# Weight rests of 100 tiles: a subtraction on GpSimd replaced by an adding transfer onto a negated copy

## The chip, the cores and the metric

The kernel runs on one core of one Trainium2 chip. The time of a kernel is the device time of one execution in microseconds; of several executions the median is given. A second number, the span, goes from the first to the last instruction that the profiler recorded. Positions "at 1490.60" are microseconds from the start of the span of the profiled execution.

The engines are TensorE (PE in the rows: matrix products; PEld: its loading of the stationary operand), VectorE (DVE), ScalarE (ACT), GpSimd (POOL) and SyncE (SP, which here issues loads). Transfers (DMAs) run on 16 DMA engines, whoever issues them.

## The reference

Two layers of a diffusion trunk work on 256 latent tokens and 256 context tokens of width 1024, all in float32. Each layer is

```python
x  = x  + 0.5 * gate * rms(swiglu(modulate(rms(x))))      # macaron half step
x  = x  + gate * rms(concat(attention, s5, conv) @ w_out) # token mixer
x  = x  + 0.5 * gate * rms(swiglu(modulate(rms(x))))      # macaron half step
```

with `swiglu(h) = (silu(h @ wg) * (h @ wu)) @ wd`, inner width 2816. Shift, scale and gate come from products of a conditioning vector with `w_ada`. The context tokens go through the same layers up to the mixer of the last one, and the latent tokens of the last layer are the output.

## The kernel before, in words

**Products in three passes.** The matmuls take float32r operands. Each float32 operand is split into a rounded part and a rest: `hi = round(w)`, `lo = w - hi`. A product of weights and activations is then three matmuls, hi x hi, hi x lo and lo x hi, summed in PSUM (`mm3`, line 148; all of its matmuls carry line 158). `mmr` does the same with the activations as the stationary operand (line 493).

**Splitting a weight tile** (`wsplit`, lines 129 to 137). A tile is 128 partitions by 1024 columns (896 or 640 for the down projection). SyncE loads it into a raw buffer `wr` (line 126). ScalarE writes the rounded part `wh` (line 133). Then the rest `wl` is subtracted on VectorE or, with `pool` set, on GpSimd (line 136). There are 4 raw buffers, 6 buffers of `wh` and 6 of `wl`; a buffer is free again when its last reader is done. So SyncE can load about four tiles ahead, and a rest can be made as soon as the matmuls of a tile six before it are over.

**Who subtracts what.** GpSimd subtracts the gate and up tiles of the first feed-forward group of a macaron step (`weights`, line 619, through `units` of the interleaved projection), the down tiles of its last group (`down`, line 667), the first eight tiles of the mixer's input projection (line 1275), all of the output projections (`weight`, line 1303, and `rows_out`, line 1338), and the gate and up tiles of the last feed-forward (`ffn_last`, from line 499). VectorE subtracts the others.

**Order of the work.** TensorE's order is written out by hand. The tokens are handled in two spans of 256 columns. A macaron step goes through four groups of inner blocks, 5, 5, 5 and 7; each makes its gated activations and then its share of the down projection. In the last group this is done span by span: when the first span is summed, its normalization begins (`boundary`, line 379, and `pre`, line 356) while TensorE goes on with the second span. In it VectorE multiplies, adds to the stream `x` (line 392, for d = 0 and 4 on GpSimd) and adds squares up (`square_acc`, line 354; ScalarE makes the squares, line 353). TensorE sums over partitions (`ss`, line 340), VectorE works out the reciprocal root on 128x1 and 128x2 columns (lines 296 to 324), TensorE spreads it (`rb`, line 333), and VectorE and ScalarE form the next sublayer's input `hh`, `hl` (lines 365 to 373). Below, the stretch from the last group of one sublayer to the dense part of the next is called a handover; there are four before the last feed-forward.

**Interleaved projection** (`skewed`). The first tiles of the next sublayer are taken in units of two. The first two units go through the eight input blocks together, block by block, so that they can start when the first block of the new input is there; the other units follow one by one. For the second span three units are still in their buffers; the first one is loaded and split again at the end.

The order of VectorE, ScalarE, GpSimd and SyncE is laid out at compile time by a list scheduler that reckons with its own durations; each engine then works in that order, and each instruction waits for the semaphores that it needs. Background streams (products with `w_ada`, the state space tables) are put between, and are paused in the handovers.

Of the kernel before, what the change touches and what calls it, by code (L numbers as in the profile page):

```python
# [8 lines left out]
F32 = mybir.dt.float32  # L9
# [3 lines left out]
AF = mybir.ActivationFunctionType  # L13
OP = mybir.AluOpType
# [17 lines left out]
RF = -27.0 / 1024  # L32
MAGIC_ROUND = 12582912.0
RAW = 4
WB = 6
FIRST = 3
SKEW_IN = 4
# [2 lines left out]
PO = (0, 1)  # L40
PI = (0, 1)
# [39 lines left out]
class Trunk:  # L81
    def __init__(self, ctx, tc, a, out):
# [7 lines left out]
        self.small = P("small", 2)  # L90
        self.wpool = P("w", WB)
        self.mm = P("mm", 6, space=PSUM)
# [31 lines left out]
    def wraw(self, src, cols=1024):  # L124
        w = self.wpool.tile([128, 1024], F32, name=self.nm("wr"), tag="wr", bufs=RAW)
        self.nc.sync.dma_start(w[:, :cols], src)
        return w

    def wsplit(self, src, cols=1024, pool=False):
        nc = self.nc  # L130
        w = self.wraw(src, cols)
        h = self.wpool.tile([128, 1024], F32R, name=self.nm("wh"), tag="wh")
        nc.scalar.activation(h[:, :cols], w[:, :cols], AF.Copy)  # L133
        lo = self.wpool.tile([128, 1024], F32R, name=self.nm("wl"), tag="wl")
        eng = nc.gpsimd if pool else nc.vector
        eng.tensor_tensor(lo[:, :cols], w[:, :cols], h.bitcast(F32)[:, :cols], op=OP.subtract)  # L136
        return h, lo

    def split(self, x, lo, hi, pool=False):
# [431 lines left out]
    def skewed(self, units, H, pend, done):  # L571
# [4 lines left out]
        for i, (span, q) in enumerate(pend):  # L576
            self.drain(q)
            lo, hi, s = span
            use = [n for n, u in enumerate(units) if s in u[1]]
            have = list(W)[-(WB // 2):] if i else []  # L580
            use = [n for n in have[::-1] if n in use] + [n for n in use if n not in have]
# [19 lines left out]
    def ffn(self, l, j, H, pend, nxt, order=None):  # L601
        nc, a = self.nc, self.a
# [3 lines left out]
        for gi, fs in enumerate(FGROUPS):  # L606
# [10 lines left out]
                nc.vector.tensor_tensor(gl[:, lo:hi], g, gh.bitcast(F32)[:, lo:hi], op=OP.subtract)  # L617

            def weights(f, pool=True):
                return [self.wsplit(a["wgu"][l, j, i, f], pool=pool and i in PI) for i in range(2)]  # L620

            def gate_up(f, ws, lo, hi, late=False):
                ps = [self.ps("pgu") for _ in range(2)]
# [5 lines left out]
            if gi == 0 and not isinstance(pend, list):  # L629
                rest = fs[FIRST:]  # L630
                new = lambda s: self.wpool.tile([128, 1024], F32R, name=self.nm(s), tag=s)
                ws = [((new("wh"), new("wl")), a["wgu"][l, j, i, f]) for f in fs[:FIRST] for i in range(2)]
                with self.in_order(*ORDERED):
                    for k, hook in enumerate(pend(H, ws)):
                        if k == 0:
                            held = [self.ps("pgu") for _ in ws]
                        for n, (p, w) in enumerate(zip(held, ws)):
                            self.mm3(p, w[0], [H[k]], 0, T, [k], k == 0, k == KD - 1)
                            hook(n)
                    self.setup2()  # L640
                for n, f in enumerate(fs[:FIRST]):
                    glu(f, held[2 * n], held[2 * n + 1], 0, T)
            elif gi == 0:
                rest = fs[SKEW_IN:]
                units = [(lambda f=f: weights(f), (0, 1)) for f in fs[:SKEW_IN]]
                self.skewed(units, H, pend, lambda n, p, span: glu(fs[n], p[:, :256], p[:, 256:], *span[:2]))
            if gi == 0:
                self.pause = False
            for f in rest:
                ws = weights(f, gi == 0 and f != fs[FIRST] * FD)  # L650
                gate_up(f, ws, *((order or spans)[0][:2] if f == NF - 1 else (0, T)))
# [4 lines left out]
            lastg = gi == len(FGROUPS) - 1  # L656
# [9 lines left out]

            def down(d):
                return self.wsplit(a["wd"][2 * l + j, d, :, fs[0] * 128:(fs[-1] + 1) * 128], n * 128,
                                   pool=lastg and d % 2 in PO)

            def downs(ds, lo, hi):

                for ks in (range(n - 1), range(n - 1, n)):
                    for d in ds:
                        if not ks.start:
                            if d not in wd:
                                wd[d] = down(d)
                            pd[d] = self.ps("pd")
                        self.mm3(pd[d], wd[d], acts[ks.start:ks.stop], lo, hi, ks, ks.start == 0, ks.stop == n)
# [13 lines left out]
            for span in order or spans:  # L693
                lo, hi, _ = span
                ds = range(KD)
                if out:
                    gate_up(fs[-1], ws, lo, hi, True)
                    ds = ds[::-1]
                    for d in ds[WB - 2:]:
                        del wd[d]  # L700
# [40 lines left out]
    def ssm_params(self):  # L741
# [25 lines left out]

        pw = self.wpool.tile([128, 1024], F32, name=self.nm("pw"), tag="wr", bufs=RAW)[:, :2 * 9 * w]
        pw = pw.rearrange("p (i k w) -> p i k w", i=2, k=9)
# [223 lines left out]
    def ssm_chunks1(self, u):  # L993
# [3 lines left out]
        for half in range(2):  # L997
            t = self.wpool.tile([128, 1024], F32, name=self.nm("ut"), tag="wr", bufs=RAW)
            for jh in range(2):
# [77 lines left out]
    def ssm_out(self, l, gh, U, S, lo):  # L1077
# [6 lines left out]
        vt = [self.wraw(self.V[l, gh, ri]) for ri in range(2)]  # L1084
        yt = self.wpool.tile([128, 1024], F32, name=self.nm("yt"), tag="wr", bufs=RAW)
        ng, r = 128 // n, 8 * n // 128
# [139 lines left out]
    def mixer(self, l, H, pend, newH):  # L1226
        nc, a = self.nc, self.a
        last = l == NL - 1
        both = self.spans
        lo = CTX if last else 0  # L1230
# [30 lines left out]
        def conv(h):  # L1261
# [5 lines left out]
            for slo, shi, _ in (both[1:] if last else both):  # L1267
# [4 lines left out]
            nc.gpsimd.tensor_tensor(o[:, lo:], o[:, lo:], ev[8 + h][:, lo:], op=OP.mult)  # L1272
            cat[4 + h] = self.split(o, lo, T)

        units = [(lambda t=t: [self.wsplit(a["w_in"][l, t + i], pool=i in PI) for i in range(2)],
                  (1,) if last and t >= 4 else (0, 1)) for t in range(0, 8, 2)]

        def done(n, p, span):
# [22 lines left out]
        wo, po, ny, H2, out = {}, {}, ([], []), [], []  # L1301

        def weight(d):
            wo[d] = self.wsplit(a["w_out"][l, d], pool=True)

        def part(d, k, s):

# [28 lines left out]
        wr, yr, us, q = {}, {}, [], []  # L1336

        def rows_out(t, h, k):

            i = [k in z for z in KPAIRS].index(True)  # L1340
            if (h, i) not in wr:
                wr[h, i] = self.wsplit(a["w_outr"][h, i], pool=True)
            p, done = yr.setdefault((t, h), ([], []))
            if not p:
                p.append(self.ps("yr"))
            self.mmr(p[0], cat[k], wr[h, i], t, KPAIRS[i].index(k) * 512, not done, len(done) == KD - 1)
            done.append(k)
# [12 lines left out]
        units = [(i, qt) for i in range(4) for qt in ((0, 1) if last else (0, 1, None))]  # L1360
# [8 lines left out]
        def early_out(n):  # L1369
            if last:  # L1370
                rows_out(n // 100, n // 10 % 10, n % 10)
            else:
                part(n // 100, n // 10 % 10, n % 10)
# [5 lines left out]
            t=tile_in, u=lambda n: ut.extend(self.ssm_chunks1(u)), U=lambda n: U.extend(self.ssm_chunks2(ut)),  # L1379
            v=lambda n: vtok(), k=lambda n: ksplit(), q=qsplit,  # L1380
            s=lambda n: S.append(self.ssm_states(l, n, U)), o=lambda n: yt.append(self.ssm_out(l, n, U, S[n], lo)),
            b=lambda n: G.append(self.ssm_back(yt[n], lo)), w=weight, r=lambda n: next(rows, None),
            g=lambda n: self.ssm_glu(l, G, cat, lo), e=early_out, x=tail if last else bound, S=attn_s,
            y=lambda n: oevac(n // 10, n % 10), z=lambda n: self.advance(out[0][1]), W=weight,
            T=lambda n: PT.update({n: self.attn_t(P.pop(n), units[n][1])}),
            V=lambda n: self.attn_pv(PT.pop(n), vt, cat, *units[n]))
# [243 lines left out]
```

## Time and profile before

| | us |
|---|---|
| median of 3 executions | 1874.86 |
| lowest, highest | 1871.24, 1876.22 |
| profiled execution, its own time | 1868.04 |
| its span | 1866.3 |

The mean granted clock of TensorE over the span is 0.963 of 2.4 GHz. The row of a group of instructions gives the line, the engine, the operation, its output and inputs by the program's names, their shapes, the number of instructions, the busy time and the mean duration of one. A row of a timeline gives start and duration and, in brackets, the idle time of the engine before it and what ended that. A row of the chain of waits gives start, duration and what the end of the program depended on in that time. The table by stretches gives, for each engine, busy microseconds in a window with the number of instructions, then TensorE's granted clock, the mean busy share of the DMA engines and what they moved.

### The profile page before, as it was taken

What the parts mean: (1) busy time and instruction counts of PE and PEld (TensorE: products, weight loads), DVE (VectorE), ACT (ScalarE), POOL (GpSimd) and SP (SyncE); (2) the same over time, 40 slices, a digit from 0 to 9 for tenths busy, and PEclk for the clock granted to TensorE, in tenths of its full rate; (3) what the DMA queues carried; (4) which work ended last, traced back from release to release, by engine and by line L of the source; (5) the groups of instructions that cost most, each with busy time, mean ns of one, the idle gap of its engine ahead of it and who ended that gap; (6) DMA issues with size and microseconds to landing.
All of it is one profiled execution on the core that took longest, in us unless ns stands there. A gap on an engine that the chain in (4) does not pass through costs nothing.

```text
span 1866.3 us, 28704 instructions
## 1 busy us (share of the span) xinstructions
PE 1728.9 (93%) x11040; PEld 1490.1 (80%) x11040; DVE 1244.4 (67%) x2204; ACT 667.2 (36%) x1181; POOL 730.6 (39%) x647
## 2 busy tenths in 40 slices
PE   7999989977997989999999979999999879889998
PEld 5887768867976889777888979888888878679997
DVE  5787877578669676767874386765456696964334
ACT  4432222224334553322222243322222334455443
POOL 4100978745354143443438353000001553436552
PEclk9999989988998989999999989999999999899999
DMA  7665556553143121655664332656466423455662
GB/s 277 223 197 170 181 154 208 192 175 102 45 154 131 34 79 47 189 182 170 199 194 156 108 102 63 209 162 199 125 203 221 125 91 120 148 163 168 190 184 91
DMA packets 103482, 285.95 MB, mean 153 GB/s; under 512 B 19904, under 2 KB 27152, under 8 KB 103344
## 3 DMA queue, kind: packets, MB, share of 16 engines
q1 hardware_dynamic: 102992, 283.91, 48.4%
q8 instruction: 87, 1.43, 0.3%
q14 instruction: 51, 0.42, 0.1%
q0 software_dynamic: 64, 0.12, 0.0%
q10 hardware_dynamic: 288, 0.07, 0.0%
HBM read 270.45 MB, written 15.70 MB: 153 GB/s over the span
## 4 chain that ended last, share of the span: by engine, by line
PE 65%; DVE 19%; POOL 6%; DMA 4%; issue 3%; ACT 2%; SPq 0%; DVEq 0%; ACTq 0%; POOLq 0%
PE pgu L158 32%; PE pd L158 14%; PE sk L158 6%; PE yr L493 4%; DMA wr<-in_w_ada_dram 3%; DVE junk L251 2%; DVE x L392 2%; DVE xacc L354 2%; PE po L158 2%; DVE bt L389 1%; DVE hl L373 1%; DVE wl L136 1%; PE ss L340 1%; PE pgu L543 1%; POOL tt L976 1%
## 5 line engine op out<-in xcount | busy, mean ns | idle before, releaser
L136 POOL TENSOR_TENSOR wl<-wr,wh 128x1024 fp32r<-128x1024 f32 (+1 forms) x140 | 334.8, 2405 | 593.3 <-ACT wh L133 280.7
L133 ACT ACTIVATE wh<-wr 128x1024 fp32r<-128x1024 f32 (+2 forms) x350 | 341.4, 980 | 601.5 <-PE pgu L158 185.4
L158 PE MATMUL pgu<-hh,wh 128*128 128x512 f32 (+1 forms) x1296 | 470.7, 363 | 0.0
L158 PE MATMUL pgu<-hl,wh 128*128 128x512 f32 (+1 forms) x1296 | 466.2, 360 | 0.0
L158 PE MATMUL pgu<-hh,wl 128*128 128x512 f32 (+1 forms) x1296 | 465.6, 359 | 0.0
L251 DVE SCALAR_TENSOR_TENSOR junk<-wr,sb 128x1024 bf16<-128x1024 f32 x224 | 306.2, 1367 | 197.5 <-DMA wr<-in_w_ada_dram 195.6
L158 PEld LDWEIGHTS pgu<-hh,wh 128*128 128x128 f32 x1296 | 245.4, 189 | 41.0 <-issue 1.7
L158 PEld LDWEIGHTS pgu<-hl,wh 128*128 128x128 f32 x1296 | 245.3, 189 | 39.5 <-issue 0.5
L158 PEld LDWEIGHTS pgu<-hh,wl 128*128 128x128 f32 x1296 | 245.1, 189 | 39.3
L136 DVE TENSOR_TENSOR wl<-wr,wh 128x1024 fp32r<-128x1024 f32 (+1 forms) x210 | 250.7, 1196 | 33.4 <-ACT wh L133 33.2
L158 PE MATMUL pd<-xh,wh 128*128 128x512 f32 (+1 forms) x696 | 244.5, 351 | 9.3 <-ACT xh L616 5.7
L158 PE MATMUL pd<-xl,wh 128*128 128x512 f32 (+1 forms) x696 | 240.8, 346 | 2.2 <-DVE xl L617 2.0
L158 PE MATMUL pd<-xh,wl 128*128 128x512 f32 (+1 forms) x696 | 240.4, 345 | 1.5 <-POOL wl L136 1.5
L158 PEld LDWEIGHTS pd<-xh,wh 128*128 128x128 f32 x696 | 135.3, 194 | 26.1 <-ACT xh L616 6.0
L158 PEld LDWEIGHTS pd<-xl,wh 128*128 128x128 f32 x696 | 135.1, 194 | 19.3 <-DVE xl L617 3.2
L158 PEld LDWEIGHTS pd<-xh,wl 128*128 128x128 f32 x696 | 135.0, 194 | 17.6 <-POOL wl L136 1.8
L158 PE MATMUL sk<-hh,wh 128*128 128x256 f32 x480 | 141.5, 295 | 0.0
L158 PE MATMUL sk<-hl,wh 128*128 128x256 f32 x480 | 138.8, 289 | 0.0
L158 PE MATMUL sk<-hh,wl 128*128 128x256 f32 x480 | 138.4, 288 | 0.0
L616 ACT ACTIVATE xh<-g 128x512 fp32r<-128x512 f32 (+1 forms) x74 | 42.6, 576 | 222.0 <-DVE g L615 221.9
L158 PEld LDWEIGHTS sk<-hh,wh 128*128 128x128 f32 x480 | 94.5, 197 | 0.3
L158 PEld LDWEIGHTS sk<-hl,wh 128*128 128x128 f32 x480 | 94.4, 197 | 0.3
(386 smaller groups left out, 2622.6 us busy)
## 6 DMA issues: line engine op xcount, KB each, us to landing
wr<-in_wgu_dram SPq DMA_DIRECT2D x170, 512.0 KB, 4.2
wr<-in_w_ada_dram SPq DMA_DIRECT2D x144, 512.0 KB, 4.4
wr<-in_wd_dram SPq DMA_DIRECT2D x72, 320.0 KB, 3.0
wr<-in_w_in_dram SPq DMA_DIRECT2D x32, 512.0 KB, 3.7
wr<-in_wd_dram SPq DMA_DIRECT2D x36, 448.0 KB, 3.4
wr<-in_wdr_dram SPq DMA_DIRECT2D x22, 512.0 KB, 3.7
wr<-in_w_out_dram SPq DMA_DIRECT2D x10, 512.0 KB, 5.2
V<-tvv SPq DMA_DIRECT2D x16, 256.0 KB, 2.4
```

Of the source, the lines that this page charges most:

```text
L133: nc.scalar.activation(h[:, :cols], w[:, :cols], AF.Copy)
L136: eng.tensor_tensor(lo[:, :cols], w[:, :cols], h.bitcast(F32)[:, :cols], op=OP.subtract)
L158: mm = lambda a_, x_, st, sp: nc.tensor.matmul(po, a_[:, c], x_[:, lo:hi], start=st, stop=sp, skip_group_check=True)
L251: self.nc.vector.scalar_tensor_tensor(self.junk, w, 1.0, self.sb[:, s], op0=OP.mult, op1=OP.mult, accum_out=self.mod[l][:, m, b, s:s + 1])
L340: self.nc.tensor.matmul(p[:, b:b + 1], t[:, lo + b * 128:lo + (b + 1) * 128], self.ones[:, 0:1], start=first and b == 0, stop=last, skip_g ...
L354: nc.vector.tensor_tensor(acc[:, lo:hi], acc[:, lo:hi], sq[:, lo:hi], op=OP.add)
L373: nc.vector.scalar_tensor_tensor(xl[:, lo:hi], t, b, xh.bitcast(F32)[:, lo:hi], op0=OP.add, op1=OP.subtract)
L389: nc.vector.scalar_tensor_tensor(t[:, lo:hi], y[d][:, lo:hi], self.pv[l][s_][:, d, s:s + 1], rb[:, :hi - lo], op0=OP.mult, op1=OP.mult)
L392: eng.tensor_tensor(x[:, lo:hi], x[:, lo:hi], t[:, lo:hi], op=OP.add)
L493: mm = lambda x_, a_, st, sp: self.nc.tensor.matmul(p, x_[:, c], a_[:, o:o + 512], start=st, stop=sp, skip_group_check=True)
L543: nc.tensor.matmul(ps[i // 2][:, o:o + 128], w[:, k * 128:k * 128 + 128], U[k][:, t * 128:t * 128 + 128], start=t + n + i % 2 == 0, stop=n ...
L616: nc.scalar.activation(gh[:, lo:hi], g, AF.Copy)
```

## The change

For the tiles above except those of the last feed-forward, ScalarE writes a second, negated rounded copy into the buffer of the rest, and a transfer issued from GpSimd reads the same weights from memory and adds them onto it: `lo = -round(w) + w`. GpSimd's subtraction falls away. The raw buffer is read by ScalarE alone.

```diff
+ACC = 2
...
         lo = self.wpool.tile([128, 1024], F32R, name=self.nm("wl"), tag="wl")
-        eng = nc.gpsimd if pool else nc.vector
-        eng.tensor_tensor(lo[:, :cols], w[:, :cols], h.bitcast(F32)[:, :cols], op=OP.subtract)
+        if pool == ACC:
+
+            nc.scalar.activation(lo[:, :cols], w[:, :cols], AF.Copy, scale=-1.0)
+            nc.gpsimd.dma_start(lo[:, :cols], src, accum_op=OP.add)
+        else:
+            eng = nc.gpsimd if pool else nc.vector
+            eng.tensor_tensor(lo[:, :cols], w[:, :cols], h.bitcast(F32)[:, :cols], op=OP.subtract)
         return h, lo
...
             def weights(f, pool=True):
-                return [self.wsplit(a["wgu"][l, j, i, f], pool=pool and i in PI) for i in range(2)]
+                return [self.wsplit(a["wgu"][l, j, i, f], pool=ACC if pool and i in PI else False) for i in range(2)]
...
                 return self.wsplit(a["wd"][2 * l + j, d, :, fs[0] * 128:(fs[-1] + 1) * 128], n * 128,
-                                   pool=lastg and d % 2 in PO)
+                                   pool=ACC if lastg and d % 2 in PO else False)
...
-        units = [(lambda t=t: [self.wsplit(a["w_in"][l, t + i], pool=i in PI) for i in range(2)],
+        units = [(lambda t=t: [self.wsplit(a["w_in"][l, t + i], pool=ACC if i in PI else False) for i in range(2)],
...
-            wo[d] = self.wsplit(a["w_out"][l, d], pool=True)
+            wo[d] = self.wsplit(a["w_out"][l, d], pool=ACC)
...
-                wr[h, i] = self.wsplit(a["w_outr"][h, i], pool=True)
+                wr[h, i] = self.wsplit(a["w_outr"][h, i], pool=ACC)
```

## Rows read from the trace of the kernel before

**Rows 1.** The page, span and busy time of three engines.
```profile
span 1866.3 us, 28704 instructions
...
PE 1728.9 (93%) x11040; PEld 1490.1 (80%) x11040; DVE 1244.4 (67%) x2204; ACT 667.2 (36%) x1181; POOL 730.6 (39%) x647
```
**Rows 2.** Stretches: width, then busy us per engine, clock, DMA share, GB/s.
```profile
385.00:516.00 131.00, 107.21 (x809) 104.88 (x810) 91.76 (x189) 48.74 (x94) 63.75 (x37) 0.88 0.32 99
586.00:760.00 174.00, 157.59 (x1207) 141.65 (x1204) 127.70 (x291) 80.87 (x190) 56.52 (x29) 0.91 0.24 74
1070.00:1168.00 98.00, 85.68 (x660) 84.33 (x659) 73.25 (x164) 38.04 (x75) 43.20 (x22) 0.93 0.26 79
1168.00:1469.00 301.00, 301.00 (x1412) 249.25 (x1411) 179.04 (x264) 87.43 (x121) 18.16 (x8) 1.00 0.58 183
1469.00:1556.00 87.00, 69.98 (x531) 68.50 (x530) 72.61 (x158) 35.73 (x71) 49.01 (x35) 0.92 0.30 91
```
**Rows 3.** Timeline of TensorE in a handover: start, us, instruction, idle before.
```profile
1490.60 0.58 PE L340 MATMUL ss<-ones,xacc 128*128 128x1 f32 x4 [4.53 <-DVE xacc L354]
```
**Rows 4.** Timeline of VectorE in the same handover.
```profile
1479.55 0.41 DVE L354 TENSOR_TENSOR xacc<-xacc,sq 128x256 f32<-128x256 f32 x1
...
1486.37 2.56 DVE L354 TENSOR_TENSOR xacc<-xacc,sq 128x256 f32<-128x256 f32 x1
```
**Rows 5.** Timeline of GpSimd in the same handover.
```profile
1481.78 6.86 POOL L136 TENSOR_TENSOR wl<-wr,wh 128x896 fp32r<-128x896 f32 x3 [0.16 <-ACT wh L133]
```
**Rows 6.** Chain of waits, 1469 to 1540: start, us, what.
```profile
1471.09 0.35 DVE t L317 x2
...
1471.89 2.12 DVE t L317 x2
...
1534.33 2.29 DVE rd L321 x2
```
**Rows 7.** Line 136 on GpSimd: durations ns min/median/max, first and last start, forms.
```profile
L136 POOL TENSOR_TENSOR wl<-wr,wh x140: 2081/2396/3320, 69.8 to 1831.3; 128x1024 fp32r<-128x1024 f32 x104, 128x896 fp32r<-128x896 f32 x36
```
**Rows 8.** Line 136 on GpSimd in the last stretch: width, busy, clock, DMA share, GB/s.
```profile
1656.00:1867.00 211.00, 95.92 (x40) 0.98 0.51 160
```
**Rows 9.** DMA queues (packets, MB, share) and issues (KB each, us to landing).
```profile
q1 hardware_dynamic: 102992, 283.91, 48.4%
...
wr<-in_w_in_dram SPq DMA_DIRECT2D x32, 512.0 KB, 3.7
wr<-in_wd_dram SPq DMA_DIRECT2D x36, 448.0 KB, 3.4
...
ident<-in_k_ident_dram ACTq DMA_DIRECT2D x1, 64.0 KB, 5.4
vec<-in_vec_dram POOLq DMA_DIRECT2D x1, 48.0 KB, 5.4
```
**Rows 10.** Timeline of ScalarE at three handovers: the roundings.
```profile
1128.63 1.06 ACT L133 ACTIVATE wh<-wr 128x1024 fp32r<-128x1024 f32 x1 [0.99 <-PE sk L158]
...
1155.72 2.01 ACT L133 ACTIVATE wh<-wr 128x1024 fp32r<-128x1024 f32 x2 [6.93 <-PE sk L158]
...
1451.83 1.79 ACT L133 ACTIVATE wh<-wr 128x896 fp32r<-128x896 f32 x2 [3.62 <-PE pd L158]
...
1500.56 1.04 ACT L133 ACTIVATE wh<-wr 128x1024 fp32r<-128x1024 f32 x1
```
**Rows 11.** Timeline of TensorE at the start of an interleaved projection.
```profile
1504.14 0.28 PE L158 MATMUL sk<-hh,wh 128*128 128x256 f32 x1
```
**Rows 12.** Chain of waits: a down projection's first half, an interleaved projection's end.
```profile
1141.56 26.70 PE sk L158 x225
...
1447.23 19.94 PE pd L158 x168
```

## The prediction, made before the changed kernel was run

> **What bounds the kernel now.** I read the page's busy shares first. TensorE is busy for 1728.9 of 1866.3 us, VectorE for 1244.4 and GpSimd for 730.6 [rows 1]: TensorE is the bound wherever it is fed, and GpSimd, as a total, is not near one. So the question is where TensorE is not fed. The table by stretches answers it [rows 2]. In the dense stretch 1168 to 1469 TensorE is busy for all 301 us; nothing done there to GpSimd can gain anything. The handovers between sublayers are different. TensorE's idle time is the width less its busy time: 23.8 us in 385 to 516, 16.4 in 586 to 760, 12.3 in 1070 to 1168, 17.0 in 1469 to 1556, together 69.5 us. The granted clock is 0.88 to 0.93 there and 1.00 in the dense stretch, so some matmuls after a pause run at the lower of the two levels (1.2 instead of 2.4 GHz).
>
> What does TensorE wait for in a handover? One row: the column sums `ss` at 1490.60 stand after 4.53 us of idle time, ended by VectorE's `xacc` [rows 3]. VectorE's own rows say why that is late: one addition into `xacc` of 128x256 takes 0.41 us at 1479.55 and the same form 2.56 us at 1486.37 [rows 4]. It ends at 1488.93; GpSimd's run of three weight subtractions covers 1481.78 to 1488.64 [rows 5]. VectorE's operation stood until GpSimd's instruction was over. In the chain of waits of 1469 to 1540 there are eleven VectorE pieces so stretched; the first is a pair of 128x1 operations at 1471.89 with 2.12 us, the last a pair at 1534.33 with 2.29, where such a pair at 1471.09 took 0.35 [rows 6]. Eleven pieces of 0.8 to 2.6 us above their short form make some 21 us on a chain that leaves TensorE idle for 17.0. So **GpSimd's subtraction costs time through VectorE**, not through its own total.
>
> **What goes.** 140 weight rests are subtracted on GpSimd, 104 of 128x1024 and 36 of 128x896, median 2.40 us [rows 7]; the 40 of the last feed-forward, after 1656, keep their code [rows 8]. So 100 subtractions go, about 236 us of GpSimd, among them all those of the four handovers. The gain is not 236 us but what VectorE's stretched steps cost TensorE: at most the 69.5 us of idle time, at least nothing. I take three quarters, 52 us: in the handover looked at, the stretches cover all the idle time, but the other stretches also hold waits of the attention, of a modulation matrix's loads and of ScalarE. Shorter pauses also give back clock: 8 us, an estimate of 2 per handover from the clock column [rows 2]. **Gain: 60 us (0 to 77).**
>
> **What comes.** Per tile: a second ScalarE activation (1.04 us for 1024 columns, 0.9 for 896 [rows 10]) and a transfer from GpSimd's queue that reads the weights from memory again and adds them onto the negated copy. No transfer of the old kernel adds, so its time from issue to landing, L, must be bounded. Nearest rows: a plain load lands in 3.7 us for 512 KB and 3.4 for 448 [rows 9]. Below: 3.7, if the adding costs nothing. One pass of 512 KB costs each DMA engine 1.7 us on average: the load queue's 48.4% of 16 x 1866.3 us, over 283.91 MB, times 0.524 MB, over 16 [rows 9]. What adds must also read what it adds to, so I take a second pass, and half a pass (0.8) for what is in front of it: L = 3.7 + 1.7 + 0.8 = 6.2 us, and 5.7 for 448 KB. Above: four passes, 9.6. GpSimd's queue itself shows no extra: its 48 KB load landed in 5.4 us, ScalarE's 64 KB load at the same time in 5.4 [rows 9]. I stay with two passes because the transfer has two inputs.
>
> The Trainium skill ("Collectives: The Full Stack", section "The bandwidth ceiling") says the same of adding transfers in reductions: the sum is free, the second source read halves the rate. By that rule L is this sum's; no run here shows it yet.
>
> Now each place where a rest becomes late, because 2.4 us of subtraction become 1.0 + L:
> (a) Down projection of each macaron step, last group, first half. 168 matmuls take 19.94 us from 1447.23 [rows 12], 2.49 per tile. The fifth tile's buffer comes free at 1451.83 [rows 10]; its rest is needed at 1457.4. Of these 5.6 us two activations take 1.8, so 3.8 are left for L = 5.7: 1.9 us, three times, 5.7.
> (b) Fourth tile of each interleaved projection. Its rounding starts at 1500.56 [rows 10], the projection at 1504.14 [rows 11]; eleven matmuls at 0.12 us (26.70 over 225 [rows 12]) later the rest is due: 4.9 us, less 2.1, leaves 2.8 for 6.2: 3.4 us, four times, 13.6.
> (c) The unit loaded again for the second half: free at 1155.72 [rows 10], due after 179 of the 225 matmuls from 1141.56 [rows 12] (33 left of the first half, 96 of two units, 48 of a third, two of its own), at 1162.8: 7.1 less 2.1 leaves 5.0: 1.2 us, three times, 3.6.
> (d) The seventh tile, in the first half: free at 1128.63 [rows 10], and before its rest is due stand nine matmuls of the first four tiles, 48 of the next two and two of its own, 7.0 us; less 2.1 leaves 4.9: 1.3 us, four times, taken half because the handover's own chain can end later: 2.6.
> (e) The output projections, 18 tiles that are asked for as soon as the attention ends: at two first uses, by the sizes of (b) to (d), 1 to 3 us each; I take 3 for both.
> (f) ScalarE: 100 more activations of about 1 us, where a handover's squares and copies queue behind them: 6 us, one in six of eight half handovers (0 to 16).
> In sum 34.5 us; each microsecond more of L costs about 13.5.
>
> Moved without a cost: SyncE's load into a raw buffer waited for the subtraction and now waits for ScalarE's second read, which ends earlier. On GpSimd's queue the rope products and the additions of d = 0 and 4 stand behind a transfer that waits for the negated copy; before, they stood behind a subtraction that waited for the rounding and then took 2.4 us more. Memory traffic grows by 50 MB (64 x 0.524 + 36 x 0.459), in stretches where the DMA share is 0.24 to 0.32 [rows 2].
>
> **Sum.** 60 - 34.5 = 25.5 us less. The profiled execution took 1868.04 us, 0.4% under the median of 1874.86: 1842.5 by its own time, 1849 by the median.
>
> **The rivals.**
> *Late rests (slower).* The adding transfer needs four passes, L = 9.6. The costs rise to 34.5 + 13.5 x 3.4 = 80 and TensorE waits for rests where it waited for VectorE: 1874.9 + 20 = 1895. It decides from L = 8.1, where 13.5 x 1.9 uses up the 25.5. For it: nothing in this trace prices an adding transfer. Against: DMA engines are idle two thirds of the time there. 0.26.
> *A plain load's speed.* L = 3.7: only (b) with 3.6 and (f) with 6 stay; 1825. 0.18.
> *Descriptors held up.* VectorE's instructions delay GpSimd's issue as GpSimd's delay VectorE's. GpSimd's subtraction varies from 2.08 to 3.32 us [rows 7]; if each transfer is held by that 1.2 us, costs are 51, the gain left is 9 and the time 1866, on the edge of measurable. 0.13, half of it counted as faster.
> The Trainium skill ("SBUF — State Buffer", section "SBUF: two separate sides") has a rule that speaks against this change: while VectorE runs in a two-port mode, GpSimd cannot write the descriptors of its transfers and they stall. By it the time is this rival's.
> *The stretch stays.* VectorE is held up by the issue of the transfers as by the subtractions; nothing is gained, the costs stay: 1909. Against it is the exact end of a stretch with the subtraction [rows 4, 5]. 0.04. That the parts cancel otherwise: 0.03. That the change doesn't act can't be: the edited calls make every one of the 100 tiles.
>
> **The numbers.** Forecast 0.36, of 1835 to 1865. Faster by over 0.3% (5.6 us, about what can be told from no change): 0.36 + 0.18 + 0.06 = 0.60; within: 0.07 + 0.03 = 0.10; slower: 0.26 + 0.04 = 0.30. The range goes from 1816 (L = 3.7 with most of the possible gain) to 1897 (four passes).
>
> **What would show it.** Right: additions into `xacc` in handovers at 0.4 us, VectorE's busy time down by about 100 us, 40 subtractions left on GpSimd, 100 additional activations, adding transfers landing in about 6 us, and short TensorE waits ended by them at the fourth tile of a projection and the fifth of a down projection. Wrong: landings over 8 us, DMA share above 0.8 in handovers, or VectorE rows still over 2 us beside an issue.

## The result, and the profile after

| | kernel before | changed kernel |
|---|---|---|
| median, us | 1873.05 (4 runs) | 1919.79 (4 runs, 1917.80 to 1921.06) |
| span of the profiled execution | 1866.3 | 1919.3 |
| TensorE busy, and idle (span less busy) | 1728.9, 137.4 | 1752.7, 166.6 |
| mean granted clock | 0.963 | 0.950 |

The change makes the kernel **slower by 46.7 us**, ratio 1.0257 (1.0242 to 1.0271). The forecast was 1849, the range ended at 1897. One execution of one kernel below, that with ScalarE's additional copy, took 2379 us at a granted clock of 0.653 and is left out of its median.

The first lines of the changed kernel's page, its DMA queues (packets, MB, share of 16 engines) and some of its DMA issues (KB each, median us to landing):

```profile
span 1919.3 us, 28880 instructions
...
PE 1752.7 (91%) x11040; PEld 1507.2 (79%) x11040; DVE 1119.3 (58%) x2204; ACT 752.4 (39%) x1281; POOL 582.9 (30%) x647
...
q1 hardware_dynamic: 102992, 283.91, 46.0%
q0 software_dynamic: 14464, 50.20, 13.7%
...
wr<-in_w_in_dram SPq DMA_DIRECT2D x32, 512.0 KB, 6.8
wr<-in_wd_dram SPq DMA_DIRECT2D x36, 448.0 KB, 5.1
wl<-in_wd_dram POOLq DMA_DIRECT2D x36, 448.0 KB, 8.5
wl<-in_wgu_dram POOLq DMA_DIRECT2D x26, 512.0 KB, 10.5
```

Against [rows 1], VectorE is busy for 125 us less, and ScalarE has its 100 additional activations. Against [rows 9], the adding transfers (queue q0) of the two largest groups land in 8.5 and 10.5 us, and the plain loads beside them in 6.8 and 5.1 us where they took 3.7 and 3.4. Instructions that write the rests (ns min/median/max; first and last start, us) and the landings of all 100 transfers:

```profile
L138 ACT ACTIVATE wl<-wr x100: 932/1041/1081, 69.5 to 1691.5; 128x1024 fp32r<-128x1024 f32 x64, 128x896 fp32r<-128x896 f32 x36
...
L142 POOL TENSOR_TENSOR wl<-wr,wh x40: 2348/2400/2597, 1709.2 to 1884.3; 128x1024 fp32r<-128x1024 f32 x40
L139 POOL DMA_DIRECT2D wl<-in_wd_dram x36: 857/866/881, 393.4 to 1524.1; - x36
...
DMA to landing us min/median/max: 5.4/9.8/15.6
```

Only the 40 subtractions of the last feed-forward are left [rows 7, 8]. In the handovers VectorE is no longer held: the additions that answer to [rows 4] take 0.41 to 0.57 us in the changed kernel's timeline. Of all 48 such additions the longest took 2.63 us before and takes 0.57 now.

```profile
1518.92 0.42 DVE L360 TENSOR_TENSOR xacc<-xacc,sq 128x256 f32<-128x256 f32 x1
1519.65 0.57 DVE L360 TENSOR_TENSOR xacc<-xacc,sq 128x256 f32<-128x256 f32 x1
1521.20 0.41 DVE L360 TENSOR_TENSOR xacc<-xacc,sq 128x256 f32<-128x256 f32 x1
```

So the mechanism that was to go is gone. What came in its place stands in the waits of TensorE (sum of us, count, longest):

```profile
PE sk L164 <- DMA wl<-in_wgu_dram: 24.7, 11, 3.3
...
PE pd L164 <- DMA wl<-in_wd_dram: 24.0, 11, 7.7
...
PE sk L164 <- DMA wl<-in_w_in_dram: 20.4, 9, 3.1
...
PE yr L499 <- DMA wl<-in_w_outr_dram: 5.8, 4, 1.8
...
PE po L164 <- DMA wl<-in_w_out_dram: 4.0, 1, 4.0
...
PE pgu L164 <- DMA wl<-in_wgu_dram: 1.8, 1, 1.8
```

37 waits with 80.7 us, each ended by the landing of a rest; the kernel before has none of them. **Why they land so late** is seen in one burst: the stretch of the third step's down projection, first in the kernel before, then in the changed one (width, busy us by engine, clock, DMA share, GB/s).

```profile
1447.00:1467.00 20.00, 20.00 (x171) 20.00 (x170) 10.49 (x16) 6.71 (x12) 11.10 (x5) 1.00 0.51 146
```

```profile
1465.00:1496.00 31.00, 24.32 (x167) 22.09 (x165) 9.78 (x20) 17.11 (x25) 6.93 (x8) 1.00 0.96 254
```

The DMA engines are at 0.96. Four adding transfers are issued there, at 1472.14, 1473.82, 1476.50 and 1478.18 on GpSimd's timeline, and this is what each one, and the plain load issued near it, took to land (issues in four windows of about 1 us each, in this order; last number: us to landing):

```profile
wr<-in_wd_dram SPq DMA_DIRECT2D x1, 448.0 KB, 4.8
wl<-in_wd_dram POOLq DMA_DIRECT2D x1, 448.0 KB, 8.5
...
wr<-in_wd_dram SPq DMA_DIRECT2D x1, 448.0 KB, 8.5
wl<-in_wd_dram POOLq DMA_DIRECT2D x1, 448.0 KB, 10.0
...
wr<-in_wd_dram SPq DMA_DIRECT2D x1, 448.0 KB, 9.2
wl<-in_wd_dram POOLq DMA_DIRECT2D x1, 448.0 KB, 10.7
...
wr<-in_wd_dram SPq DMA_DIRECT2D x1, 448.0 KB, 10.8
wl<-in_wd_dram POOLq DMA_DIRECT2D x1, 448.0 KB, 11.4
```

Each is later than the one in front of it. ScalarE releases one every 2.0 us on average ((1478.18 - 1472.14) / 3); one takes 2.6 us of every DMA engine (13.7% of 1919.3 us, over 100), and the plain loads of the next tiles come on top. That is more than the engines can serve. The first step's burst looks the same (share 1.04 from 401 to 425, by the packets that start there, against 0.40 from 401 to 421 before). Over the whole kernel, the 62 transfers that are issued within 4 us of the one before land in 10.6 us in the median, the 22 that come 10 us or more after it in 7.4: a transfer with another close in front of it lands some 3 us later.

### The profile page after: what moved, and what is told of

Its sections match the earlier page's. It is cut to its first block, busy times and chain, and to the rows that moved or that the text cites. A ratio compares the mean times of both kernels' runs of the same rounds, so it can differ in the third digit from the quotient of the medians.

```text
span 1919.3 us, 28880 instructions
## 1 busy us (share of the span) xinstructions
PE 1752.7 (91%) x11040; PEld 1507.2 (79%) x11040; DVE 1119.3 (58%) x2204; ACT 752.4 (39%) x1281; POOL 582.9 (30%) x647
## 3 DMA queue, kind: packets, MB, share of 16 engines
q0 software_dynamic: 14464, 50.20, 13.7%
## 4 chain that ended last, share of the span: by engine, by line
PE 46%; DMA 8%; issue 8%; DVE 5%; ACT 2%; POOL 1%; DVEq 0%; POOLq 0%; ACTq 0%; SPq 0%
PE pgu L164 24%; PE pd L164 10%; PE yr L499 3%; PE sk L164 3%; DMA wl<-in_wgu_dram 2%; PE po L164 2%; DMA wl<-in_wd_dram 1%; DMA wl<-in_w_out_dram 1%; DMA wl<-in_w_in_dram 1%; ACT wl L138 1%; PE pgu L549 1%; ACT wh L134 1%; DMA wr<-in_w_outr_dram 1%; POOL wl L139 1%; DMA wglu<-in_w_glu_dram 1%
## 5 line engine op out<-in xcount | busy, mean ns | idle before, releaser
L257 DVE SCALAR_TENSOR_TENSOR junk<-wr,sb 128x1024 bf16<-128x1024 f32 x224 | 297.1, 1326 | 207.2 <-DMA wr<-in_w_ada_dram 205.5
L164 PE MATMUL sk<-hh,wl 128*128 128x256 f32 x480 | 148.2, 309 | 45.1 <-DMA wl<-in_wgu_dram 24.7
L139 POOL DMA_DIRECT2D wl<-in_wd_dram x36 | 31.2, 867 | 443.4 <-ACT wl L138 435.5
L164 PE MATMUL sk<-hh,wh 128*128 128x256 f32 x480 | 148.3, 309 | 0.0
L164 PE MATMUL sk<-hl,wh 128*128 128x256 f32 x480 | 144.9, 302 | 0.0
L164 PEld LDWEIGHTS sk<-hh,wl 128*128 128x128 f32 x480 | 101.1, 211 | 49.5 <-DMA wl<-in_wgu_dram 27.2
L142 POOL TENSOR_TENSOR wl<-wr,wh 128x1024 fp32r<-128x1024 f32 x40 | 95.9, 2400 | 79.3 <-ACT wh L134 78.4
L622 ACT ACTIVATE xh<-g 128x512 fp32r<-128x512 f32 (+1 forms) x74 | 42.5, 574 | 184.1 <-DVE g L621 184.0
## 6 DMA issues: line engine op xcount, KB each, us to landing
wl<-in_wgu_dram POOLq DMA_DIRECT2D x26, 512.0 KB, 10.5
```

The source lines that it names most:

```text
L139: nc.gpsimd.dma_start(lo[:, :cols], src, accum_op=OP.add)
L164: mm = lambda a_, x_, st, sp: nc.tensor.matmul(po, a_[:, c], x_[:, lo:hi], start=st, stop=sp, skip_group_check=True)
L257: self.nc.vector.scalar_tensor_tensor(self.junk, w, 1.0, self.sb[:, s], op0=OP.mult, op1=OP.mult, accum_out=self.mod[l][:, m, b, s:s + 1])
L622: nc.scalar.activation(gh[:, lo:hi], g, AF.Copy)
```

## The experiments

All times are medians beside runs of the kernel before on the same chip; differences are against those.

### What the subtraction's going is worth

**The changed kernel without the transfer.** The rests of the 100 tiles stay the negated copy.

```diff
             nc.scalar.activation(lo[:, :cols], w[:, :cols], AF.Copy, scale=-1.0)
-            nc.gpsimd.dma_start(lo[:, :cols], src, accum_op=OP.add)
```

> The changed kernel without its adding transfers: the buffer of the rest keeps the negated rounded copy that ScalarE writes, so the products of the weight rests are those of another number (this part of the computation is replaced). Late rests: all of the loss hangs on the transfers, and without them the freed VectorE shows: before (1873) less 60 plus 6 for ScalarE, 1819, at least under 1840. ScalarE's activations: the loss stays, 1900 or more. No gain from the freed VectorE: 1873 to 1880, and VectorE's additions in the handovers at 0.4 us change nothing.

1805.38 us, ratio 0.9648 (0.9626 to 0.9671): 65.7 us faster. The first lines of its page:

```profile
span 1803.6 us, 28594 instructions
...
PE 1708.7 (95%) x11040; PEld 1471.5 (82%) x11040; DVE 1120.0 (62%) x2204; ACT 751.5 (42%) x1281; POOL 492.0 (27%) x547
```

TensorE's idle time falls by 42.5 us (137.4 to 94.9), and its busy time by 20.2 for the same 11040 matmuls: the mean granted clock is 0.979. The gain that was forecast is there, and the rest of the story is the transfer's.

**The kernel before with ScalarE's additional copy** in the 100 tiles, over which GpSimd's subtraction then writes.

```diff
         h = ...
+            nc.scalar.activation(lo[:, :cols], w[:, :cols], AF.Copy, scale=-1.0)
             nc.gpsimd.tensor_tensor(lo[:, :cols], w[:, :cols], h.bitcast(F32)[:, :cols], op=OP.subtract)
```

> The kernel before with ScalarE's negated copy added: GpSimd then writes the rest over it by its subtraction. Only ScalarE's 100 activations are new. Late rests: 6 to 15 us over before, 1879 to 1888. ScalarE's activations as the cause of the loss: 1915 or more.

1878.11 us, ratio 1.0036 (1.0020 to 1.0053): ScalarE's part costs 7 us. If the two add up, the subtraction's going alone is worth some 73.

**The kernel before with GpSimd's subtraction in pieces**, in halves and in quarters (all 140 of them, the last feed-forward's too).

```diff
-        eng.tensor_tensor(lo[:, :cols], w[:, :cols], h.bitcast(F32)[:, :cols], op=OP.subtract)
+        n = 4 if pool else 1
+        for c in range(n):
+            z = slice(c * cols // n, (c + 1) * cols // n)
+            eng.tensor_tensor(lo[:, z], w[:, z], h.bitcast(F32)[:, z], op=OP.subtract)
```

> The kernel before with each of GpSimd's 140 subtractions cut into two of half the columns. VectorE waits for the end of the instruction that it meets: its stretches halve to about 1 us and about half of the 66 us that the freed VectorE is worth comes back, 1840 (1830 to 1855). VectorE is simply met twice as often: no change, 1871 within 6 us.

> The kernel before with each of GpSimd's weight subtractions in four quarters. Theory (a two-input VectorE operation stands until GpSimd's instruction is over, so a shorter instruction holds it shorter): two halves gave 19 us, quarters should give more, 1835 to 1852. Rival (VectorE is held anew by each piece, or each piece adds its own overhead to GpSimd, which was 769 us with halves against 731): no gain over halves, 1852 to 1875.

Halves: 1853.65 us, ratio 0.9908 (0.9891 to 0.9925). Quarters: **1823.97 us, ratio 0.9742 (0.9726 to 0.9759)**, better than both kernels compared here and than the range expected. The fourth addition into `xacc` of the same handover, 2.56 us in the kernel before [rows 4], on VectorE's timeline with halves and then with quarters:

```profile
1475.39 1.35 DVE L357 TENSOR_TENSOR xacc<-xacc,sq 128x256 f32<-128x256 f32 x1
```

```profile
1486.24 0.96 DVE L357 TENSOR_TENSOR xacc<-xacc,sq 128x256 f32<-128x256 f32 x1
```

The hold, above the 0.41 of an addition left alone, is 2.15, 0.94 and 0.55 us; GpSimd's median piece is 2.40, 1.29 and 0.74 us. The hold follows the length of GpSimd's instruction, which shows the mechanism as a series and not only by its absence. The longest of all 48 such additions goes the same way, 2.63, 1.52 and 0.96 us, and each of the three additions ends 0.28 to 0.29 us after a subtraction or piece of GpSimd's (1488.93 after 1488.64; 1476.74 after 1476.46; 1487.20 after 1486.91). GpSimd itself is busy for 98 us more with quarters (828.6 against 730.6), and that costs nothing that shows.

**The 100 subtractions on VectorE**, without a transfer or a second activation (the five calls pass `pool=False`).

> The kernel before with the 100 subtractions on VectorE, 1.19 us each there, no transfer and no second ScalarE activation. Theory (what GpSimd's subtraction cost was its hold on VectorE, 125 us of VectorE's busy time, so VectorE doing the 119 us of work itself comes out about even in total, but in no operation of the handover chain is a hold of 2 us left): 1840 to 1870. Rival (in the handovers VectorE is the engine of the chain, and the subtractions stand in its queue ahead of the sums): 1880 to 1920.

1840.39 us, ratio 0.9825 (0.9810 to 0.9841). So VectorE's own 1.2 us per tile cost less here than the holds did.

### What the transfer costs

**A plain copy in place of the adding one.** Every engine executes the same instructions in the same order; the rests of the 100 tiles are the weights.

```diff
-            nc.gpsimd.dma_start(lo[:, :cols], src, accum_op=OP.add)
+            nc.gpsimd.dma_start(lo[:, :cols], src)
```

> The transfers from GpSimd's queue copy the weights instead of adding them (the rest is then the weight itself, another number in the same products). One pass instead of two for each. Late rests by the engines' time: landing falls from 10 to about 6 us and the time, at 13.5 us for each microsecond, to about 1866. Late rests by the software queue's own start: landing stays over 8 us and the time over 1895.

1825.22 us, ratio 0.9750 (0.9729 to 0.9772). The same bytes without the adding save 92.6 us (46.7 + 45.9, each against the kernel before beside it). The landings came down to about 6 us, as engine time alone would have it; the time came out 41 us under the 1866 that was worked out from them. Its landings and the share of its GpSimd queue:

```profile
DMA to landing us min/median/max: 4.1/5.8/9.0
```

```profile
q0 software_dynamic: 14464, 50.20, 7.8%
```

In DMA time: 13.7% of 1919.3 us with the addition, 7.8% of 1822.7 without, 263 against 142 us of every engine, a factor of 1.85.

**Every second transfer adds, the others copy** (their calls pass another value than `ACC`), in the same order again; and **each transfer adds only the first half of the columns**, with some VectorE and ScalarE instructions in another order.

```diff
-            nc.gpsimd.dma_start(lo[:, :cols], src, accum_op=OP.add)
+            nc.gpsimd.dma_start(lo[:, :cols], src, **({'accum_op': OP.add} if pool == ACC else {}))
```

```diff
-            nc.gpsimd.dma_start(lo[:, :cols], src, accum_op=OP.add)
+            nc.gpsimd.dma_start(lo[:, :cols // 2], src[:, :cols // 2], accum_op=OP.add)
```

> As the changed kernel, but only every second of the 100 transfers adds; the others copy the weights over the negated copy, so half of the rests are the weights themselves. Every engine executes the same instructions in the same order as the changed kernel and as the kernel in which all 100 copy. Theory (the transfers are served by the same engines, so that each waits for what is in front of it): the adding ones land well below the 8.5 to 10.5 us they take when all add, some 7.5 to 8.5, and the copies above the 5.1 to 6.3 they take when all copy, some 6.5 to 7.5; the time lies at or under the mean of 1919.8 and 1825.2, 1850 to 1875. Rival (an adding transfer takes its own fixed time, whatever is beside it): landings stay 8.5 to 10.5 and 5.1 to 6.3, and the time, set by the later rest of each pair, stays over 1890.

> As the changed kernel, but each transfer adds only the first half of the columns; the second half of each of the 100 rests stays the negated copy. As many transfers, issues and ScalarE copies, half of the bytes. Some VectorE and GpSimd instructions change places, since the scheduler reckons with a shorter transfer. Theory (the price is the DMA engines' time): two passes over half the bytes are what one pass over all of them is, so landings of 5 to 6.5 us as for the plain copies, and a time of 1820 to 1840. Rival (adding has a price of its own per transfer, such as reading what it adds to before it can write): landings stay over 8 us and the time over 1870.

Alternating: 1874.66 us, ratio 1.0017 (1.0000 to 1.0034), about the mean of the two kernels that it mixes (1872.5). Half the columns: 1838.22 us, ratio 0.9824 (0.9796 to 0.9853). The landings of the 100 transfers of the one, then of the other:

```profile
DMA to landing us min/median/max: 4.2/8.1/11.6
```

```profile
DMA to landing us min/median/max: 3.9/6.6/8.8
...
q0 software_dynamic: 14464, 25.16, 7.9%
```

The second kernel rules out a fixed price of the adding as the main part: as many adding transfers with half the bytes land in 6.6 us instead of 9.8, with the DMA time of the plain copies (7.9% against 7.8%). In the first kernel, with the two kinds told apart by their issue on GpSimd (0.87 and 0.53 us), the 50 that add land in 8.6 us in the median, where they took 9.8 among adding ones, and the 50 copies in 7.7, where they took 5.8 among copies: each kind's landing depends on what is beside it. For the time it says less: the mean that theory gave as its upper end is what was measured. The series, each line from one profiled execution but for the difference of medians (the one with half the columns was 9 us above its median, the one with every second adding 7):

| 100 transfers | landing, us | DMA time of q0 | TensorE idle | TensorE busy | against before |
|---|---|---|---|---|---|
| none | - | - | 94.9 | 1708.7 | -65.7 |
| plain copies | 5.8 | 7.8% | 102.7 | 1720.0 | -45.9 |
| half the columns add | 6.6 | 7.9% | 117.7 | 1728.0 | -33.9 |
| every second adds | 8.1 | 10.7% | 141.1 | 1738.5 | +2.6 |
| all add (the change) | 9.8 | 13.7% | 166.6 | 1752.7 | +46.7 |

From a landing of 5.8 to 9.8 us, a microsecond costs 23 us ((46.7 + 45.9) / 4): 16 of idle time and 8 of busy time.

**Every second tile keeps the negated copy, with no transfer at all**; and **every second tile keeps GpSimd's subtraction** (`True` in place of `NEG`). One of five calls:

```diff
-... self.wsplit(a["wgu"][l, j, i, f], pool=ACC if pool and i in PI else False) ...
+... self.wsplit(a["wgu"][l, j, i, f], pool=(ACC if i else NEG) if pool and i in PI else False) ...
```

> Every second of the 100 tiles gets its adding transfer, the others keep ScalarE's negated copy as their rest (another number in their products). The transfers queue behind each other: landing of a 512 KB one falls from 10.5 to under 8.5 us, and the loss against the kernel without transfers (1805) falls to much less than half of 114 us: 1835 or less. Each transfer is slow by itself: landing stays near 10 us and the loss halves, 1862.

> Adding transfers for every second of the 100 tiles, GpSimd's subtraction for the others: the reference's result is computed. The transfers queue behind each other, so half of them cost far less than half: 1805 + 25 for the transfers + 33 for half of the stretches, about 1863. Each part in proportion: 1895, the mean of before and after.

1861.36 us, ratio 0.9960 (0.9944 to 0.9976), with landings of 7.6 us in the median against 9.8: transfers do wait for each other, but most of the 9.8 us is left with half of them, and the time came out linear in their number, near the mean of none and all (1862.6), and not under 1835. The other: 1899.75 us, ratio 1.0157 (1.0142 to 1.0172): 30.1 us slower, where half of the change would be 23.4, and no way out. Both were misses for the view that thinning the transfers would free them altogether. A lone adding transfer is late too: 7.4 us in the median of the 22 above, and not one of the 100 lands in under 5.4.

**Two kernels that settled less.** In one, the transfer adds into memory that nobody reads; in the other, matmuls take the rounded copy in place of the rest.

```diff
+            un = self.dram.tile([128, 1088], F32, name=self.nm("un"))
-            nc.gpsimd.dma_start(lo[:, :cols], src, accum_op=OP.add)
+            nc.gpsimd.dma_start(un[:, :cols], src, accum_op=OP.add)
```

```diff
             nc.gpsimd.dma_start(lo[:, :cols], src, accum_op=OP.add)
+            return h, h
```

> The adding transfers go to scratch rows in memory that nothing reads; the rest is the negated copy as in the first of these kernels. Traffic and GpSimd's issuing stay nearly as in the changed kernel, but no matmul waits for a landing. Late rests: within 15 us of the kernel without transfers, about 1830. Slowed weight loads (the plain loads beside the transfers land in 6.8 us instead of 3.7): the loss stays, 1890 or more.

> All transfers and copies as in the changed kernel, but the matmuls of the 100 tiles take the rounded part also where they took the rest (another number in the same products), so TensorE waits for no landing; buffers, traffic and GpSimd's queue stay. Late rests: the time falls to that of the kernel without transfers (1805) plus 5 to 20 us. Traffic, slower weight loads: 1870 or more.

The first took 2030.63 us, ratio 1.0850 (1.0829 to 1.0871), and says nothing of late rests: with nothing to hold them, all 100 transfers were scheduled into the first 265 us, where GpSimd's queue stood behind them and TensorE behind GpSimd. It does bear out the price: 2.65 us per adding transfer when they follow each other without a pause, here into memory.

The second took 1882.39 us, ratio 1.0063 (1.0048 to 1.0078). By what was expected before it ran, that is the rival's side (traffic, slower weight loads: 1870 or more): no matmul waits for the landing of a rest, yet it is 78 us slower than the kernel without transfers. But ScalarE and GpSimd work in another order in it, and TensorE loses its time elsewhere: its waits for ScalarE's `xh` are 25.6 us there, 4.3 without transfers and none in the changed kernel, where 80.7 us of waits end with the landing of a rest. So transfers can cost as much by other ways than the matmul that reads the rest; which ones is argued and not shown (buffers that come free later, slower plain loads, work that stands behind in order). The changed kernel's loss shows at the rests in its trace, but what part of it began with the plain loads in front of them can't be told from these runs.

## Why the prediction was wrong

**What bounds the kernel: right.** VectorE's operations stood behind GpSimd's subtractions, and TensorE behind VectorE. The series of pieces shows it, as does the kernel without transfers. (The chain of [rows 6] has twelve stretched VectorE pieces by a recount, not eleven, some 22 us and not 21, which changes nothing.)

**The gain, 60 us (0 to 77): right in its mechanism, and a little low.** Less ScalarE's 6 the forecast was 54; the kernel without transfers gives 65.7. Of its parts, idle time was put at 52 and gave 42.5, clock at 8 and gave 20.2 (both with ScalarE's cost in them), so that the sum fits better than its parts, which is luck. ScalarE's term, 6, measured 7.

**Two passes: right in size.** The factor in DMA time is 1.85; that a second read is what costs it is not shown by any run. The Trainium skill ("Collectives: The Full Stack", section "The bandwidth ceiling") has the second source read halving the rate; the factor agrees nearly.

**The step that failed: L = 3.7 + 1.7 + 0.8 = 6.2 us, in its last term, "half a pass (0.8) for what is in front of it".** Measured: 10.5 us for 512 KB (the largest group) and 8.5 for 448 KB, where 6.2 and 5.7 stood. The first two terms, 5.4 us, held: the shortest landing of 512 KB is 5.5. What is in front thus measured 5.1 us and not 0.8 (3.6 for 448 KB). The prediction gives no row for the term; it goes with the mean DMA share of 0.24 to 0.32 over stretches of 87 to 174 us [rows 2], by which the added traffic was put at no cost and on which rests the argument against the rival, "DMA engines are idle two thirds of the time there". The transfers don't spread over such a stretch. ScalarE releases them in bursts while SyncE reloads the raw buffers for the next tiles, and those plain loads become late too (`w_in`: 6.8 us for 3.7). In the burst shown above the share was 0.51 before and 0.96 after, and each landing was later than the last. Where the transfers were cheap enough to land near the forecast L, the price of the places came out near the forecast as well: half the columns, 6.6 us, cost 31.8 us more than no transfer, where 28.5 (34.5 less ScalarE's 6) were forecast for 6.2. That is in part luck, since some of the 31.8 is clock, which the list did not have.

**The price of lateness: the idle part right, the clock left out.** At 13.5 us per microsecond of L, and 3.6 us more of it (9.8 for 6.2), the list (a) to (e) gives 28.5 + 48.6 = 77 us of idle time. Against the kernel without transfers TensorE's idle time grew by 71.7 (166.6 less 94.9), and its waits for rests add up to 80.7. They are not all where the list had them: 37 waits and not some 14, presumably since tiles that had a margin at 6.2 us had none at 9.8, so that the near agreement of the sums is in part luck. But TensorE's busy time grew as well, by 44.0 us (1752.7 less 1708.7), at a granted clock of 0.950 against 0.979. The gain had a term for the clock, the costs had none. Busy time times granted clock is 1665 in the changed kernel and 1673 without transfers, so the longer busy time is the lower clock. Most of it lies in the interleaved projections: their three forms of matmul (`sk`) are busy for 441.4 us in place of 410.7, longer by 30.7, also the form that reads no rest (first without transfers, then the changed kernel; busy us, mean ns, idle before), and the down projections are longer by 6.6.

```profile
L163 PE MATMUL sk<-hh,wh 128*128 128x256 f32 x480 | 138.2, 288 | 0.0
```

```profile
L164 PE MATMUL sk<-hh,wh 128*128 128x256 f32 x480 | 148.3, 309 | 0.0
```

**The sum.** Forecast: 54 us of gain less 28.5 for the transfers, 25.5 faster. Measured: 65.7 less 112.4, 46.7 slower. The gain was 11.7 better, the transfers 83.9 worse, of which, by the profiled executions, about half is idle time from the larger L (71.7 less 28.5) and half the clock (44.0).

**The rivals.** *Late rests* had the direction and the L (9.6), with the wrong reason for it: not four passes, but two and a queue. Its 1895 is 25 us short: the clock is missing, and the larger gain makes up for part of it. *Stretch stays* is out [rows 4 against the additions of 0.4 to 0.6 us]. *Descriptors held up*: the 36 issues of the `wd` transfers took 857 to 881 ns (all 100 at most 919), so no hold of 1.2 us shows on GpSimd; what the Trainium skill ("SBUF — State Buffer", section "SBUF: two separate sides") says of stalled descriptors is not seen in these rows, and wasn't tried by itself. *A plain load's speed* is what the plain copies cost, and even they landed in 5.8 us, not 3.7.

What stays open: how much of the idle time comes through late buffers and late plain loads, and not only through the transfer that the matmul waits for.

## What to carry to other kernels

When work moves from an engine to a transfer, take the DMA share in the few microseconds in which the transfers will be issued, after whatever releases them, and compare the interval between releases with the DMA time of one; a mean over the stretch hides a queue. Price a new TensorE wait twice, as idle time and as the lower clock granted afterwards (here 72 and 44 us). Where GpSimd holds VectorE up, cutting GpSimd's instruction into quarters shortened the hold shown from 2.15 to 0.55 us at no cost that shows (ratio 0.9742), before any engine or transfer was asked to do the work.

## What was not expected of the hardware

- The hold on a two-input VectorE operation scales with GpSimd's single instruction, 2.15, 0.94 and 0.55 us for pieces of 2.40, 1.29 and 0.74 us: VectorE gets in between two pieces.
- A plain copy issued by GpSimd took 0.53 us of GpSimd, an adding one 0.87, for the same shape.
- Adding transfers slow the plain loads beside them: `w_in` loads landed in 6.8 us against 3.7 before, and in 4.4 beside plain copies of the same size.
